# A top-k search cut into rounds: the search for the best keys is dealt out between chunks of projections, and the index scores move ahead of the first keys

## The chip, the cores and the metric

The kernel runs on one core of one Trainium2 chip. The metric is device time in microseconds (us); the time before is the median of three runs, and one further execution was recorded by the hardware profiler. The engines are PE (TensorE: matrix products, with PEld for its weight loads), DVE (VectorE), ACT (ScalarE), POOL (GpSimd) and SP (the queue that issues nearly all loads). Each engine works through its own list of instructions in order, and semaphores hold an instruction until its inputs are there. So one instruction that waits holds everything behind it on its engine.

## The reference

One decoder block on 256 tokens of 1024 channels. A normalised input is projected to queries, keys and values of 8 heads, to 8 small index heads, to the two halves of a gated mixer, and to two gates; attention looks only at the 64 best keys of each query; then follow a merge, an output projection and a mixture of 32 experts, two for each token.

```python
xn = rms_norm(h, norm1_g[l]); proj = xn @ w_in[l]
q, k, v, qi, ki, wi, su, sv, ga, gb = split_columns(proj)
...
rel = jax.nn.relu(jnp.einsum('bqhd,bsd->bqhs', qib, ki))
score = jnp.einsum('bqh,bqhs->bqs', wb, rel)             # index scores
score = jnp.where(causal[None], score, -jnp.inf)
_, sel = lax.top_k(score, top_k)                         # top_k = 64
logits = jnp.einsum('bqhd,bqkhd->bhqk', qb, kg) * (HEAD_DIM ** -0.5)
p = jax.nn.softmax(logits, axis=-1)                      # over the chosen keys
y_attn = jnp.einsum('bhqk,bqkhd->bqhd', p, vg)
...
h = h + merged @ w_out[l]
h = h + hier_moe(rms_norm(h, norm2_g[l]), ...)           # 32 experts, 2 a token
return rms_norm(h, norm_f_g)
```

## The kernel before

The weights of the first part come as 85 chunks of 512 KB or less, in one fixed order (`weight_chunks`): the index keys and index queries, the first half of the values (four pieces, v0.0 to v0.3), two pairs of key and query chunks (k0, k1, q0, q1, k2, k3, q2, q3), the second half of the values (v1.0 to v1.3), the other two pairs, and so on. Loads go through SP into four landing buffers taken in turn, so a load is issued when the chunk four places ahead of it has been read.

Products are taken at nearly full fp32 accuracy from three products of a coarser type. For that each chunk is split: ACT copies it into a rounded part (`hi`, a CAST), DVE subtracts to get the rest (`lo`, written `hl<-raw,hl` at L173 or L291). PE multiplies `hi` with the two parts of the input (L204, L205, for values L228, L229), then `lo` with the first (L209, for values L231). A key or query chunk is 16 products with `hi` and then 8 with `lo`; a piece of values is two halves of 4 and 2. There are three accumulators of PSUM for these products, used in turn.

After a pair of chunks DVE turns the accumulator by the position (`heads`: `ra`, `rs`, then two writes of `kt` or `qt`). The index side has its own: `index_queries(0)` and `(1)` (four copies `sw` on ACT, then three operations on DVE), the index products (`query_by_key` with `kip`, tile `lg<-index`, four groups for four pairs of index heads), a relu on ACT for each head (`rel`), and two fused multiply-adds on DVE for each head (`score`). Each row of the score has 256 keys, or 128 for the first 128 queries.

The search takes the 64 best by eight rounds. A round is, for each half of the tokens, MAX (the 8 largest of a row) and MATCH_REPLACE (these 8 crossed out), so four instructions on DVE (MATCH_REPLACE shows in the trace with a short load of its own). From what is crossed out comes `bias`, which masks the logits. `weights(p)` is the attention of heads 2p and 2p+1: products `lg<-kt,qt`, bias, softmax on DVE and ACT. `turn(p)` transposes the result on PE, `mix(p)` multiplies it with the values.

A scheduler orders each engine's instructions from the order of the program and its own estimate of times, so the order on an engine is not quite that of the code.

After the attention come the gates and mixer (to 260 us), the output projection, and from about 299 us the experts, whose 96 MB come through a ring of 23 buffers. Of these buffers many lie where the first part had its tiles, and can be filled only when that part is through.

Of the kernel before, what the change touches and what calls it, by code (L numbers as in the profile page):

```python
# [9 lines left out]
F32 = mybir.dt.float32  # L10
# [3 lines left out]
AF = mybir.ActivationFunctionType  # L14
ALU = mybir.AluOpType
# [10 lines left out]
IH = 8  # L26
TOPK = 64
# [9 lines left out]
DONE = -3.3e38  # L37
# [3 lines left out]
RELUS = 2  # L41
# [13 lines left out]
C_TRI, C_TRIL, C_CB, C_END = 172, 300, 428, 812  # L55
# [27 lines left out]
PIECES = 4  # L83
# [45 lines left out]
def block(ctx, tc, a, out):  # L129
    nc = tc.nc  # L130
# [41 lines left out]
    copies = []  # L172
# [40 lines left out]

    two = lambda n, p: [f"{n}{2 * p}", f"{n}{2 * p + 1}"]

    def tokens_by_cols(name, b, xs, between=None, **engines):

        accs = [ps.tile([P, BLOCK], F32, name="acc", bufs=3) for _ in range(NT)]
        for j in range(PIECES):
            piece = f"{name}{b}.{j}"  # L220
            if piece not in ready:
                prepare(piece, **engines)
            hi, lo = ready.pop(piece)
            for t in range(NT):
                s = slice(t * P, (t + 1) * P)
                ks = [(i, j * KD // PIECES + i) for i in range(KD // PIECES)]
                for i, k in ks:
                    mm(accs[t], xs[0][:, k, s], hi[:, i], start=(k == 0), stop=False)  # L228
                    mm(accs[t], xs[1][:, k, s], hi[:, i], start=False, stop=False)  # L229
                for i, k in ks:  # L230
                    mm(accs[t], xs[0][:, k, s], lo[:, i], start=False, stop=(k == KD - 1))  # L231
            if j == PIECES // 2 - 1 and between:
                between()
        return accs

    def scaled(dst, name, b, xs, scale, between=None, **engines):
# [47 lines left out]
    ident = con[:, C_ID:C_ID + P]  # L284
# [121 lines left out]
    def index_queries(j):  # L406
        ra, rs = rope64(qi_acc[j], swap(qi_acc[j], 2, P), 2, P)
        vec(nc.vector.tensor_add, qit[:, 2 * j:2 * j + 2], ra, rs)

    def values(b, between=None, **engines):  # L410

        v = at.tile([P, NT, BLOCK], F32, name="v", bufs=2)
        scaled(v, "v", b, xs, rstd1, between, **engines)
        return v

    def heads(p, what, between=None):

        acc = cols_by_tokens(two(what, p), xs, between)
        ra = sm.tile([P, 2, T], F32, name="ra", tag="ra", bufs=2)
        rs = sm.tile([P, 2, T], F32, name="rs", tag="rs", bufs=2)  # L420
        bc = lambda t: t[:, 0:1].broadcast_to([P, 2, T])
        nc.vector.tensor_mul(ra, acc, bc(cos))
        nc.vector.tensor_mul(rs, acc, bc(sin))
        o = at.tile([P, 2, T], F32, name=what + "t", tag=what, bufs=2)
        nc.vector.tensor_sub(o[:, 0], ra[:, 0], rs[:, 1])
        nc.vector.tensor_add(o[:, 1], ra[:, 1], rs[:, 0])
        return o

    v, kt, qt = {}, {}, {}
    v[0] = values(0, lambda: index_queries(0), act=act, vec=vec)  # L430
    index_queries(1)
    wi = at.tile([P, NT, IH], F32, name="wi")
    wi_ps = ps.tile([P, NT, IH], F32, name="wi_ps", tag="pt", bufs=2)
    for t in range(NT):
        nc.tensor.transpose(wi_ps[:, t], wit[:, t * P:(t + 1) * P], ident[0:IH, 0:IH])
    nc.scalar.copy(wi, wi_ps)
    kt[0] = heads(0, "k")

    pool(nc.gpsimd.tensor_copy, ident_b, ident)
    pool(nc.gpsimd.tensor_copy, bits[:, 2 * P:], early(C_TRI, 2 * P))  # L440

# [5 lines left out]
    def query_by_key(lhs, rhs):  # L447

        lgs = [ps.tile([P, 3 * P], F32, name="lg", bufs=2) for _ in range(2)]
        n, turn = lhs.shape[1], in_turn()  # L450
        for t in range(NT):
            for h in range(n):
                for j, lg in ((1, lgs[1]), (0, lgs[0])):
                    rows = slice(64 * j, 64 * j + 64)
                    turn(mm, lg[:, row[t]], lhs[rows, h, t * P:(t + 1) * P], rhs[rows, h, 0:(t + 1) * P],
                       start=(h == 0), stop=(h == n - 1), tile_position=(64 * j, 0))
        return lgs

    for hd in range(IH):
        if hd % 2 == 0:  # L460
            lgs = query_by_key(qit[:, hd // 2:hd // 2 + 1], kip)
        lg = lgs[hd % 2]
        rel = at.tile([P, 3 * P], F32, name="rel", tag="pts", bufs=2)
        ins = nc.scalar.activation(rel, lg, AF.Relu)
        if hd < RELUS:
            copies.append((order.index("k1"), ins))
        for t in range(NT):
            nc.vector.scalar_tensor_tensor(
                score[:, row[t]], rel[:, row[t]], wi[:, t, hd:hd + 1], (cb if hd == 0 else score)[:, row[t]],
                op0=ALU.mult, op1=ALU.add)  # L470

    work = at.tile([P, 3 * P], F32, name="work", tag="pr", bufs=2)
    for r in range(TOPK // 8):
        for t in range(NT):
            src = (work if r else score)[:, row[t]]
            m8 = at.tile([P, 8], F32, name="m8", bufs=2)
            nc.vector.max(m8, src)
            nc.vector.match_replace(work[:, row[t]], m8, src, DONE)
    bias = at.tile([P, 3 * P], F32, name="bias")
    nc.vector.tensor_tensor(bias, work, score, ALU.is_equal)  # L480
    nc.vector.scalar_tensor_tensor(bias, bias, -1.0e38, cb, op0=ALU.mult, op1=ALU.add)


    yah = big("y_hi", [P, H, T], "yah", F32R)
# [39 lines left out]
    def gating_values(b, between=None):
        scaled(sv[:, :, b * BLOCK:(b + 1) * BLOCK], "sv", b, xs, rstd1, between)

    qt[0] = heads(0, "q")
    kt[1] = heads(1, "k")
    qt[1] = heads(1, "q")
    weights(0)  # L530
    v[1] = values(1, lambda: turn(0))
    kt[2] = heads(2, "k", lambda: mix(0))
    weights(1)
    qt[2] = heads(2, "q")
    turn(1)
# [568 lines left out]
```

## Time and profile before

| | |
|---|---|
| median of three runs | 501.32 us (499.56 to 501.77) |
| profiled execution, its own time | 505.71 us |
| its span in the profile | 503.9 us |
| PE, DVE, ACT busy | 452.2, 220.3, 185.9 us |
| loads from memory | 148.88 MB, 298 GB/s over the span |
| mean granted clock of PE | 0.96 |

The span is from the first to the last instruction of the recorded execution. Its own time is 1.8 us more, and 4.4 us above the median of the runs that were only timed. Busy times of different engines overlap, so what counts is which engine is waited for in which stretch.

### The profile page before, as it was taken

How to read it: one execution, taken by the hardware profiler on the slowest of the kernel's cores; microseconds unless marked ns; L12 is line 12 of the kernel's file. 1: busy time of each engine (PE TensorE's matmuls, PEld its weight loads, DVE VectorE, ACT ScalarE, POOL GpSimd, SP SyncE). 2: the span in 40 equal slices, each digit the busy share in tenths (PEclk: the TensorE clock that was granted, in tenths of full speed). 3: DMA queues.
4: the chain of work that ended last, by engine and by line, in shares of the span. 5: the costliest groups of instructions: out<-in, count | busy, mean ns of one | idle time of the engine just before them, and what ended most of it. 6: DMA issues, size and time to landing. Idle time of an engine off the chain costs nothing.

```text
span 503.9 us, 8336 instructions
## 1 busy us (share of the span) xinstructions
PE 452.2 (90%) x3371; PEld 329.2 (65%) x3372; DVE 220.3 (44%) x416; ACT 185.9 (37%) x323; POOL 25.8 (5%) x50
## 2 busy tenths in 40 slices
PE   9999969999999999999999988989889887859581
PEld 8978968998878889988889963534435423214240
DVE  5587897667537546764656452012011000001012
ACT  7574317365487353544445541010100101000122
POOL 0030000000000000000001420000000000000010
PEclk9999979999999999999999999999999997978896
DMA  8676135956877999556689599999999999999942
GB/s 282 230 215 190 43 119 147 353 204 237 290 250 227 336 348 342 192 186 197 178 318 337 198 375 411 420 421 421 420 421 421 419 422 420 421 421 420 423 186 88
DMA packets 29134, 150.52 MB, mean 299 GB/s; under 512 B 3618, under 2 KB 4002, under 8 KB 16931
## 3 DMA queue, kind: packets, MB, share of 16 engines
q1 hardware_dynamic: 28512, 148.89, 78.0%
q10 hardware_dynamic: 578, 1.05, 0.7%
q8 instruction: 28, 0.46, 0.4%
q14 instruction: 16, 0.12, 0.1%
HBM read 148.88 MB, written 1.05 MB: 298 GB/s over the span
## 4 chain that ended last, share of the span: by engine, by line
PE 59%; DMA 23%; DVE 9%; ACT 6%; issue 2%; POOL 0%; POOLq 0%; DVEq 0%; ACTq 0%; SPq 0%
DMA rg<-in_ein 12%; PE acc L228 8%; PE acc L231 8%; PE acc L229 8%; DMA rg<-in_eout 8%; PE hd L901 6%; PE acc L209 5%; PE acc L204 4%; PE acc L205 4%; PE sum L291 3%; PE yp L291 3%; DMA raw_wo<-in_w 2%; PE xp L815 2%; DVE hl L173 2%; PE lg L291 1%
## 5 line engine op out<-in xcount | busy, mean ns | idle before, releaser
L901 PE MATMUL hd<-rg,xe 128*32 128x512 f32 x512 | 62.9, 612 | 13.4 <-DMA rg<-in_ein 12.5
L204 PE MATMUL acc<-xh,hl 128*128 128x256 f32 x224 | 56.7, 290 | 0.0
L205 PE MATMUL acc<-xl,hl 128*128 128x256 f32 x224 | 55.5, 285 | 0.0
L820 DVE TENSOR_TENSOR xe<-xp,g2t 128x256 f32<-128x256 f32 x32 | 12.2, 420 | 90.8 <-PE xp L815 69.2
L228 PE MATMUL acc<-hl,xh 128*128 128x512 f32 x128 | 51.0, 398 | 0.8 <-DVE ra L291 0.8
L229 PE MATMUL acc<-hl,xl 128*128 128x512 f32 x128 | 50.2, 392 | 0.0
L901 PEld LDWEIGHTS hd<-rg,xe 128*32 128x32 f32 x512 | 13.8, 110 | 47.7 <-issue 31.2
L204 PEld LDWEIGHTS acc<-xh,hl 128*128 128x128 f32 x224 | 43.4, 194 | 1.5 <-issue 1.0
L205 PEld LDWEIGHTS acc<-xl,hl 128*128 128x128 f32 x224 | 43.3, 193 | 0.5 <-issue 0.3
L291 PE MATMUL yp<-rg,aT 128*32 128x256 f32 (+1 forms) x528 | 35.3, 413 | 7.7 <-ACT aT L846 4.7
L836 ACT ACTIVATE act<-hd,r 128x256 f32<-128x256 f32 x8 | 3.8, 473 | 103.9 <-PE hd L901 103.9
L231 PE MATMUL acc<-hl,xh 128*128 128x512 f32 x128 | 39.4, 391 | 0.0
L209 PE MATMUL acc<-xh,hl 128*128 128x256 f32 x224 | 33.8, 295 | 0.0
L291 PE MATMUL sum<-ye,aT 128*128 128x512 f32 (+1 forms) x76 | 31.3, 552 | 1.8 <-ACT ye L927 1.8
L291 PEld LDWEIGHTS yp<-rg,aT 128*32 128x32 f32 x528 | 16.6, 119 | 23.2 <-issue 7.1
L209 PEld LDWEIGHTS acc<-xh,hl 128*128 128x128 f32 x224 | 30.5, 202 | 1.2 <-DVE hl L173 0.7
L815 PEld LDWEIGHTS <-hb 128*128 128x128 bf16 x384 | 21.9, 98 | 11.6 <-issue 11.2
L228 PEld LDWEIGHTS acc<-hl,xh 128*128 128x128 f32 x128 | 24.1, 188 | 6.6 <-issue 1.9
L231 PEld LDWEIGHTS acc<-hl,xh 128*128 128x128 f32 x128 | 24.0, 188 | 5.4 <-DVE hl L291 0.3
L229 PEld LDWEIGHTS acc<-hl,xl 128*128 128x128 f32 x128 | 24.1, 188 | 4.7
L837 DVE SCALAR_TENSOR_TENSOR act<-hd,r,act 128x256 f32<-128x256 f32 x8 | 3.9, 484 | 52.0 <-ACT act L836 52.0
L927 ACT COPY ye<-yp 128x512 f32<-128x512 f32 (+2 forms) x21 | 10.0, 482 | 41.0 <-PE yp L291 41.0
(263 smaller groups left out, 779.2 us busy)
## 6 DMA issues: line engine op xcount, KB each, us to landing
rg<-in_ein SPq DMA_DIRECT2D x64, 1024.0 KB, 19.8
rg<-in_eout SPq DMA_DIRECT2D x31, 1024.0 KB, 19.8
raw_v<-in_w SPq DMA_DIRECT2D x8, 512.0 KB, 3.7
raw_k<-in_w SPq DMA_DIRECT2D x8, 512.0 KB, 4.6
raw_q<-in_w SPq DMA_DIRECT2D x8, 512.0 KB, 4.4
raw_sv<-in_w SPq DMA_DIRECT2D x8, 512.0 KB, 4.1
raw_gb<-in_w SPq DMA_DIRECT2D x8, 512.0 KB, 5.0
raw_wb<-in_w SPq DMA_DIRECT2D x8, 512.0 KB, 5.7
```

What stands on the lines that cost most here:

```text
L173: plain = lambda f, *args, **kw: f(*args, **kw)
L204: mm(o, hi[:, k], xs[0][:, k], start=(k == 0), stop=False)
L205: mm(o, hi[:, k], xs[1][:, k], start=False, stop=False)
L209: mm(o, lo[:, k], xs[0][:, k], start=False, stop=(k == KD - 1))
L228: mm(accs[t], xs[0][:, k, s], hi[:, i], start=(k == 0), stop=False)
L229: mm(accs[t], xs[1][:, k, s], hi[:, i], start=False, stop=False)
L231: mm(accs[t], xs[0][:, k, s], lo[:, i], start=False, stop=(k == KD - 1))
L291: last.append(f(*args, **kw))
L815: mm(xp[:, k], hb[:, n, t, (q * 4 + k) * P:(q * 4 + k + 1) * P], s[:, t], start=(t == n == 0), stop=(t == NT - 1 and n == 2))
L820: nc.vector.tensor_mul(xe[:, ks], xp[:, k:k + 2], g2b)
L901: mm(hd[js[j]], xe[:, k, js[j]], w[:, j], start=(k == 0), stop=(k == KD - 1), tile_position=(0, j * CAP))
L927: nc.scalar.copy(ye[:, cs], yp)
```

## The change

The index scores become a function `scores(p)` for a pair of index heads, and the search a function `best(rounds)`. `values` and `tokens_by_cols` take a dictionary of what to do after which piece. The calls are then written in another order: `index_queries(0)` after piece v0.0, the index weights after v0.1, `index_queries(1)` after v0.2, the scores between v0, k0 and k1, and one or two rounds of the search between any two chunks from q0 to v1.1. The attention steps follow later by about a pair of chunks at first and catch up at the end; keys and queries get three buffers each in place of two.

```diff
-            if j == PIECES // 2 - 1 and between:
-                between()
+            if j in between:
+                between[j]()
...
-        o = at.tile([P, 2, T], F32, name=what + "t", tag=what, bufs=2)
+        o = at.tile([P, 2, T], F32, name=what + "t", tag=what, bufs=3)
...
-    v[0] = values(0, lambda: index_queries(0), act=act, vec=vec)
-    index_queries(1)
...
-    kt[0] = heads(0, "k")
...
-    for hd in range(IH):
-        if hd % 2 == 0:
-            lgs = query_by_key(qit[:, hd // 2:hd // 2 + 1], kip)
-        lg = lgs[hd % 2]
...
+    def scores(p):
+        for j, lg in enumerate(query_by_key(qit[:, p:p + 1], kip)):
+            hd = 2 * p + j
+            rel = at.tile([P, 3 * P], F32, name="rel", tag="pts", bufs=2)
+            ins = nc.scalar.activation(rel, lg, AF.Relu)
...
+    v[0] = values(0, {0: lambda: index_queries(0), 1: index_weights, 2: lambda: index_queries(1)}, act=act, vec=vec)
+    for p in (0, 1):
+        scores(p)
+    kt[0] = heads(0, "k", lambda: scores(2))
+    scores(3)
...
-    for r in range(TOPK // 8):
-        for t in range(NT):
-            src = (work if r else score)[:, row[t]]
-            m8 = at.tile([P, 8], F32, name="m8", bufs=2)
-            nc.vector.max(m8, src)
-            nc.vector.match_replace(work[:, row[t]], m8, src, DONE)
...
+    def best(rounds):
+        for r in rounds:
+            for t in range(NT):
+                src = (work if r else score)[:, row[t]]
+                m8 = at.tile([P, 8], F32, name="m8", bufs=2)
+                nc.vector.max(m8, src)
+                nc.vector.match_replace(work[:, row[t]], m8, src, DONE)
+        if r == TOPK // 8 - 1:
+            nc.vector.tensor_tensor(bias, work, score, ALU.is_equal)
+            nc.vector.scalar_tensor_tensor(bias, bias, -1.0e38, cb, op0=ALU.mult, op1=ALU.add)
...
-    qt[0] = heads(0, "q")
-    kt[1] = heads(1, "k")
-    qt[1] = heads(1, "q")
-    weights(0)
-    v[1] = values(1, lambda: turn(0))
-    kt[2] = heads(2, "k", lambda: mix(0))
+    qt[0] = heads(0, "q", lambda: best([0]))
+    best([1])
+    kt[1] = heads(1, "k", lambda: best([2]))
+    best([3])
+    qt[1] = heads(1, "q", lambda: best([4]))
+    best([5])
+    v[1] = values(1, {0: lambda: best([6]), 1: lambda: best([7]), 3: lambda: weights(0)})
+    kt[2] = heads(2, "k")
+    turn(0)
     weights(1)
-    qt[2] = heads(2, "q")
-    turn(1)
-    kt[3] = heads(3, "k", lambda: mix(1))
+    qt[2] = heads(2, "q", lambda: mix(0))
+    kt[3] = heads(3, "k", lambda: turn(1))
     weights(2)
-    qt[3] = heads(3, "q")
+    qt[3] = heads(3, "q", lambda: mix(1))
     turn(2)
     mixed = []
-    gating_values(0, lambda: mix(2))
-    weights(3)
-    gating_values(1, lambda: turn(3))
-    mixed.append(mix(3))
+    gating_values(0, {0: lambda: weights(3), 1: lambda: mix(2)})
+    gating_values(1, {0: lambda: turn(3), 2: lambda: mixed.append(mix(3))})
```

On DVE, the end of the search before (`m8` the eight largest, `work` the row being crossed out, hl_771 the `lo` of chunk k3, hl_808 that of q2):

```order
L477 MAX m8_663<-work_620 128x8
L477 MAX m8_666<-work_620 128x8
L478 MATCH_REPLACE work_620<-m8_663,work_620 128x128
L478 MATCH_REPLACE work_620<-m8_666,work_620 128x256
L422 TENSOR_TENSOR ra_734<-acc_675,cos_315 128x512
L480 TENSOR_TENSOR bias_669<-work_620,score_563 128x384
L423 TENSOR_TENSOR rs_735<-acc_675,sin_316 128x512
L481 SCALAR_TENSOR_TENSOR bias_669<-bias_669,con2_159 128x384
L425 TENSOR_TENSOR qt_738<-ra_734,rs_735 128x256
L426 TENSOR_TENSOR qt_738<-ra_734,rs_735 128x256
L173 TENSOR_TENSOR hl_771<-raw_k3_772,hl_771 128x1024
L173 TENSOR_TENSOR hl_808<-raw_q2_809,hl_808 128x1024
```

The same place on DVE now (hl_739 is the `lo` of k3, hl_782 that of q2):

```order
L484 MATCH_REPLACE work_620<-m8_733,work_620 128x128
L422 TENSOR_TENSOR ra_690<-acc_625,cos_315 128x512
L423 TENSOR_TENSOR rs_691<-acc_625,sin_316 128x512
L484 MATCH_REPLACE work_620<-m8_736,work_620 128x256
L425 TENSOR_TENSOR qt_694<-ra_690,rs_691 128x256
L426 TENSOR_TENSOR qt_694<-ra_690,rs_691 128x256
L173 TENSOR_TENSOR hl_739<-raw_k3_740,hl_739 128x1024
L483 MAX m8_775<-work_620 128x8
L483 MAX m8_778<-work_620 128x8
L484 MATCH_REPLACE work_620<-m8_775,work_620 128x128
L484 MATCH_REPLACE work_620<-m8_778,work_620 128x256
L173 TENSOR_TENSOR hl_782<-raw_q2_783,hl_782 128x1024
```

Before, all eight rounds stood ahead of the turning of q0 and q1 and of the `lo` of k3; now three rounds stand ahead of them, and the others behind, one or less between two subtractions.

On PE, the first attention products before, which stand between the `hi` products and the `lo` products of k3 and q2:

```order
L205 MATMUL acc<-xl,hl 128x256
L291 MATMUL lg<-kt,qt 128x128 x4
L291 MATMUL lg<-kt,qt 128x256 x2
L209 MATMUL acc<-xh,hl 128x256 x16
L204 MATMUL acc<-xh,hl 128x256
```

On PE now, at the end of v1 (one of the eight products of `weights(0)` stands a little earlier, in v1.1):

```order
L231 MATMUL acc<-hl,xh 128x512 x2
L291 MATMUL lg<-kt,qt 128x128 x3
L291 MATMUL lg<-kt,qt 128x256 x4
L204 MATMUL acc<-xh,hl 128x256
L205 MATMUL acc<-xl,hl 128x256
```

The first attention products moved behind q3 and the four pieces of v1, and nothing stands between `hi` and `lo` of k3 and q2 any more.

On ACT, in the first half of the values, before (raw_v0 are its pieces, `sw` the copies for the index queries):

```order
L291 CAST hl_402<-raw_v0_403 128x1024
L291 CAST hl_419<-raw_v0_420 128x1024
L291 COPY sw_436<-acc_244 32x512 x4
L291 CAST hl_445<-raw_v0_446 128x1024
L291 CAST hl_462<-raw_v0_463 128x1024
L291 COPY sw_481<-acc_336 32x512 x4
L173 CAST hl_496<-raw_k0_497 128x1024
```

And now:

```order
L291 CAST hl_404<-raw_v0_405 128x1024
L291 COPY sw_421<-acc_244 32x512 x4
L291 CAST hl_430<-raw_v0_431 128x1024
L173 CAST hl_525<-raw_k0_526 128x1024
L291 COPY wi_399<-wi_ps_447 128x16
L291 CAST hl_451<-raw_v0_452 128x1024
L291 COPY sw_468<-acc_336 32x512 x4
L291 CAST hl_477<-raw_v0_478 128x1024
```

The first copies `sw` moved ahead of piece v0.1, the second ahead of v0.3, and the CAST of k0, with the copy of the index weights, now stands ahead of pieces v0.2 and v0.3.

## Rows read from the trace of the kernel before

**Rows 1.** Windows in us: each engine's busy time, PE's clock, loads.

```profile
core 0: us, PE busy (x) PEld busy (x) DVE busy (x) ACT busy (x) POOL busy (x), PEclk, DMA share, GB/s
27.21:45.55 18.34, 17.53 (x100) 14.69 (x98) 13.56 (x14) 11.18 (x16) 3.03 (x3) 1.00 0.71 208
45.55:54.63 9.08, 8.92 (x58) 6.26 (x57) 7.23 (x17) 3.85 (x8) 0.00 (x0) 1.00 0.42 124
...
64.26:68.27 4.01, 0.12 (x2) 0.03 (x1) 4.01 (x13) 0.00 (x0) 0.00 (x0) 0.91 0.00 0
68.27:77.67 9.40, 9.40 (x57) 8.29 (x57) 7.21 (x10) 2.62 (x3) 0.00 (x0) 0.68 0.66 214
77.67:89.52 11.85, 11.85 (x57) 9.74 (x56) 9.58 (x17) 9.50 (x20) 0.00 (x0) 1.00 0.49 141
...
150.00:260.00 110.00, 110.00 (x597) 95.65 (x596) 66.84 (x75) 55.53 (x66) 0.89 (x2) 1.00 0.75 256
...
374.00:475.00 101.00, 78.31 (x734) 33.04 (x734) 9.92 (x28) 8.96 (x17) 1.84 (x3) 0.91 1.01 421
```

**Rows 2.** Timeline of PE: start, duration, line, tile, count, [idle before, releaser].

```profile
56.54 1.12 PE L209 MATMUL acc<-xh,hl 128*128 128x256 f32 x8
...
59.42 1.12 PE L209 MATMUL acc<-xh,hl 128*128 128x256 f32 x8
...
68.27 2.08 PE L291 MATMUL lg<-kt,qt 64*128 64x128 f32 x12 [3.89 <-DVE qt L425]
70.28 3.78 PE L209 MATMUL acc<-xh,hl 128*128 128x256 f32 x16
```

**Rows 3.** Timeline of DVE from the last scores to the subtractions behind the search.

```profile
54.86 1.40 DVE L468 SCALAR_TENSOR_TENSOR score<-rel,wi,score 128x128 f32<-128x128 f32 x4 [1.07 <-ACT rel L464]
56.18 0.61 DVE L477 MAX8 m<-score 128x8 f32<-128x128 f32 x2
...
65.57 0.69 DVE L422 TENSOR_TENSOR ra<-acc,cos 128x512 f32<-128x512 f32 x1
66.17 0.56 DVE L480 TENSOR_TENSOR bias<-work,score 128x384 f32<-128x384 f32 x1
...
67.70 0.42 DVE L425 TENSOR_TENSOR qt<-ra,rs 128x256 f32<-128x256 f32 x1
...
68.37 1.23 DVE L173 TENSOR_TENSOR hl<-raw_k,hl 128x1024 fp32r<-128x1024 f32 x1
69.50 2.36 DVE L173 TENSOR_TENSOR hl<-raw_q,hl 128x1024 fp32r<-128x1024 f32 x2
```

**Rows 4.** Timeline of PE around the first group of index products.

```profile
44.59 1.12 PE L209 MATMUL acc<-xh,hl 128*128 128x256 f32 x8
45.64 0.93 PE L291 MATMUL lg<-index 64*128 64x128 f32 x8
46.50 0.38 PE L204 MATMUL acc<-xh,hl 128*128 128x256 f32 x1
```

**Rows 5.** Timeline of PE in the first half of the values.

```profile
30.68 0.47 PE L228 MATMUL acc<-hl,xh 128*128 128x512 f32 x1 [0.81 <-DVE ra L291]
...
37.58 0.61 PE L231 MATMUL acc<-hl,xh 128*128 128x512 f32 x2
...
38.94 0.61 PE L231 MATMUL acc<-hl,xh 128*128 128x512 f32 x2
```

**Rows 6.** SP issues k0 and k1; landing of k0 alone; the page's median.

```profile
28.16 2.00 SPq L167 DMA_DIRECT2D raw_k<-in_w  x2
...
DMA to landing us min/median/max: 3.5/3.5/3.5
...
raw_k<-in_w SPq DMA_DIRECT2D x8, 512.0 KB, 4.6
```

**Rows 7.** Timeline of ACT: four copies for the index queries, and one CAST.

```profile
33.42 2.35 ACT L291 COPY sw<-acc 32x512 f32<-32x512 f32 x4
...
47.37 1.05 ACT L173 CAST hl<-raw_k 128x1024 fp32r<-128x1024 f32 x1
```

More of the change, by code (lines that the diff above doesn't have):

```diff
@@ L214, in block, with tokens_by_cols @@
     two = lambda n, p: [f"{n}{2 * p}", f"{n}{2 * p + 1}"]
-    def tokens_by_cols(name, b, xs, between=None, **engines):
+    def tokens_by_cols(name, b, xs, between={}, **engines):
         accs = [ps.tile([P, BLOCK], F32, name="acc", bufs=3) for _ in range(NT)]
@@ L231, in tokens_by_cols, with scaled @@
                     mm(accs[t], xs[0][:, k, s], lo[:, i], start=False, stop=(k == KD - 1))
-            if j == PIECES // 2 - 1 and between:
-                between()
+            if j in between:
+                between[j]()
         return accs
-    def scaled(dst, name, b, xs, scale, between=None, **engines):
+    def scaled(dst, name, b, xs, scale, between={}, **engines):
         for t, acc in enumerate(tokens_by_cols(name, b, xs, between, **engines)):
@@ L408, in index_queries, with values @@
         vec(nc.vector.tensor_add, qit[:, 2 * j:2 * j + 2], ra, rs)
-    def values(b, between=None, **engines):
+    def values(b, between={}, **engines):
         v = at.tile([P, NT, BLOCK], F32, name="v", bufs=2)
@@ L427, in heads, with index_weights @@
         return o
-    v, kt, qt = {}, {}, {}
-    v[0] = values(0, lambda: index_queries(0), act=act, vec=vec)
-    index_queries(1)
     wi = at.tile([P, NT, IH], F32, name="wi")
-    wi_ps = ps.tile([P, NT, IH], F32, name="wi_ps", tag="pt", bufs=2)
-    for t in range(NT):
-        nc.tensor.transpose(wi_ps[:, t], wit[:, t * P:(t + 1) * P], ident[0:IH, 0:IH])
-    nc.scalar.copy(wi, wi_ps)
-    kt[0] = heads(0, "k")
-    pool(nc.gpsimd.tensor_copy, ident_b, ident)
-    pool(nc.gpsimd.tensor_copy, bits[:, 2 * P:], early(C_TRI, 2 * P))
+    def index_weights():
+        wi_ps = ps.tile([P, NT, IH], F32, name="wi_ps", tag="pt", bufs=2)
+        for t in range(NT):
+            nc.tensor.transpose(wi_ps[:, t], wit[:, t * P:(t + 1) * P], ident[0:IH, 0:IH])
+        act(nc.scalar.copy, wi, wi_ps)
     row = (slice(0, P), slice(P, 3 * P))
@@ L457, in query_by_key @@
         return lgs
-    for hd in range(IH):
-        if hd % 2 == 0:
-            lgs = query_by_key(qit[:, hd // 2:hd // 2 + 1], kip)
-        lg = lgs[hd % 2]
[L463 to L470, printed above, removed]
@@ L472, in block @@
-    work = at.tile([P, 3 * P], F32, name="work", tag="pr", bufs=2)
-    for r in range(TOPK // 8):
-        for t in range(NT):
-            src = (work if r else score)[:, row[t]]
-            m8 = at.tile([P, 8], F32, name="m8", bufs=2)
-            nc.vector.max(m8, src)
-            nc.vector.match_replace(work[:, row[t]], m8, src, DONE)
-    bias = at.tile([P, 3 * P], F32, name="bias")
-    nc.vector.tensor_tensor(bias, work, score, ALU.is_equal)
-    nc.vector.scalar_tensor_tensor(bias, bias, -1.0e38, cb, op0=ALU.mult, op1=ALU.add)
+    def scores(p):
[3 more added lines that the diff above has]
+            ins = nc.scalar.activation(rel, lg, AF.Relu)
+            if hd < RELUS:
+                copies.append((order.index("k1"), ins))
+            for t in range(NT):
+                nc.vector.scalar_tensor_tensor(
+                    score[:, row[t]], rel[:, row[t]], wi[:, t, hd:hd + 1], (cb if hd == 0 else score)[:, row[t]],
+                    op0=ALU.mult, op1=ALU.add)
@@ new lines, in block @@
+    v, kt, qt = {}, {}, {}
+    v[0] = values(0, {0: lambda: index_queries(0), 1: index_weights, 2: lambda: index_queries(1)}, act=act, vec=vec)
[3 more added lines that the diff above has]
+    scores(3)
+    pool(nc.gpsimd.tensor_copy, ident_b, ident)
+    pool(nc.gpsimd.tensor_copy, bits[:, 2 * P:], early(C_TRI, 2 * P))
+    work = at.tile([P, 3 * P], F32, name="work", tag="pr", bufs=2)
+    bias = at.tile([P, 3 * P], F32, name="bias")
+    def best(rounds):
+        for r in rounds:
+            for t in range(NT):
+                src = (work if r else score)[:, row[t]]
[5 more added lines that the diff above has]
+            nc.vector.scalar_tensor_tensor(bias, bias, -1.0e38, cb, op0=ALU.mult, op1=ALU.add)
@@ L522, in block, with gating_values @@
     sv = big("m_hi", [P, NT, D], "sv")
-    def gating_values(b, between=None):
+    def gating_values(b, between={}):
         scaled(sv[:, :, b * BLOCK:(b + 1) * BLOCK], "sv", b, xs, rstd1, between)
-    qt[0] = heads(0, "q")
-    kt[1] = heads(1, "k")
-    qt[1] = heads(1, "q")
-    weights(0)
-    v[1] = values(1, lambda: turn(0))
-    kt[2] = heads(2, "k", lambda: mix(0))
+    qt[0] = heads(0, "q", lambda: best([0]))
[7 more added lines that the diff above has]
+    turn(0)
     weights(1)
-    qt[2] = heads(2, "q")
-    turn(1)
-    kt[3] = heads(3, "k", lambda: mix(1))
+    qt[2] = heads(2, "q", lambda: mix(0))
+    kt[3] = heads(3, "k", lambda: turn(1))
     weights(2)
-    qt[3] = heads(3, "q")
+    qt[3] = heads(3, "q", lambda: mix(1))
     turn(2)
     mixed = []
-    gating_values(0, lambda: mix(2))
-    weights(3)
-    gating_values(1, lambda: turn(3))
-    mixed.append(mix(3))
+    gating_values(0, {0: lambda: weights(3), 1: lambda: mix(2)})
+    gating_values(1, {0: lambda: turn(3), 2: lambda: mixed.append(mix(3))})
     ta.close()
```

## Prediction

> **What bounds the kernel now.** I read the windows first, to find the stages and their limits. In the last long one, 374 to 475 us, the DMA engines are full (share 1.01, 421 GB/s) and PE is not (78 of 101 us): the experts' weights set that end. From 150 to 260 us it is the other way: PE is busy for all 110 us and loads run at 256 GB/s, so they wait for buffers that PE's progress frees [rows 1]. A microsecond won on PE before 150 us therefore moves everything behind it, the start of the full stream too.
>
> So I looked for what PE loses before 90 us. There is one hole: from 64.26 to 68.27 PE has 0.12 us of work, while DVE is busy for all 4.01 us [rows 1]. In PE's timeline the hole ends with the products `lg<-kt,qt`, released by the write of `qt` on DVE [rows 2]. DVE's timeline says why `qt` is late: from 56.18 to 65.57 it does nothing but the eight rounds, 9.39 us, and the turning of q0 and q1 and the subtractions for k3 and q2 stand behind them [rows 3]. The hole has a tail: in the 9.40 us behind it the granted clock is 0.68 [rows 1], and sixteen `lo` products take 3.78 us where eight took 1.12 [rows 2].
>
> **What is removed.** Four terms, all on PE.
> - The hole: 4.0 us.
> - The slow clock behind it: 9.40 x (1 - 0.68) = 3.0 us. It was at the lower level (1.2 in place of 2.4 GHz) for most of that stretch, after the idle, and came back with work.
> - Scattered index products. Between the last `lo` product ahead of the first group (44.59 + 8 x 0.12 = 45.55) and the next chunk's first product at 46.50 lie 0.95 us [rows 4]: one group in one piece. A chunk takes 59.42 - 56.54 = 2.88 us [rows 2]. Four groups and one chunk should take 4 x 0.95 + 2.88 = 6.7 us; the window 45.55 to 54.63 holds just these and took 9.08 [rows 1]: 2.4 us lost, since three groups are cut up among the products of q0.
> - The 0.81 us that PE waited in v0 for the index queries to leave their accumulator [rows 5].
>
> Together 10.2 us: the most that this change can give.
>
> **What is added.** No instruction is new, so the price is in waits; I followed the new lists with the durations of the rows.
>
> *First half of the values* (two steps of 1.36 us make a piece of 2.72 [rows 5]). The second accumulator of v0 is free once the index queries' multiplications are through: about 0.25 us of waiting at 28.6, where 0.81 was. The subtraction of v0.1 now stands behind these three operations: 0.25 at 31.2. Then ACT. Its CAST of k0 stands ahead of that of v0.2. The load of k0 is issued at 28.16 and landed 3.5 us later [rows 6], so the CAST (1.05 us [rows 7]) is over at 32.7; the copy of the index weights waits for their transposes on PE, to 33.7; v0.2 is ready at 34.8. PE has the weights and one index group to do meanwhile, to 34.5: 0.3 us of waiting. If k0 took the median of 4.6 us [rows 6], it would be 0.5. Then the four copies `sw`, 2.35 us [rows 7], stand ahead of v0.3: ready at 38.2, wanted at 37.75, so 0.45. Together 1.25 us. The load of q1 now waits for the subtraction of v0.3, near 40.7; its CAST then ends near 46, ahead of relus wanted by PE at 48.2, so this is covered; were it 2 us later, the next index group would wait that long.
>
> *The search.* Before, DVE's list held eight rounds in one block; now its work from the end of k1 must keep pace with PE. In my count k1 ends at 48.2 on PE and DVE is free at 48.55. Until the `lo` of v1.0 stands: three turnings at 0.60 x 2 for `ra`, `rs` and 0.67 for the writes (66.17 - 65.57 and 68.37 - 67.70), five subtractions at 1.13 (69.50 - 68.37), four multiply-adds at 0.33 (56.18 - 54.86 for four), six rounds at 9.39 / 8 = 1.17 [rows 3]: 5.6 + 5.65 + 1.3 + 7.0 = 19.6 us, that is 68.2. PE does one index group and six chunks, 0.95 + 17.3 us, to 66.5, and wants that `lo` after four products, 0.9 us on: it waits 0.8. For q3 the same count gives 0.25, for k3, q2 and the other pieces of v1 0.1 or less. Together 1.1 us. Here DVE and PE have almost the same amount of work, so any delay of DVE is PE's.
>
> How a round fares when it is cut by other instructions the trace does not show. Below, it could be free of cost, even with the waits of 1.1 gone. Above, I take one wait like the 1.07 us for the relu [rows 3] at each of two places, 2.1 us, and the clock falling once, 3.0. I take no extra, since within the block each instruction already followed the one it needs.
>
> *Pieces.* The second index group is split 3 + 1, and the products of `weights(1)` are cut by transposes: 0.3 us each, estimated from the 2.4 us lost on three cut groups. `weights(0)` goes from 6 + 2 to 1 + 7: nothing. SP issues the same loads; only k2's stands ahead of q0's and some expert pieces one load earlier. That is covered by four landing buffers: PE takes 4 x 2.88 us to come round to one. The later `weights`, `turn` and `mix` still have two chunks or pieces between softmax and transposes: nothing.
>
> Sum: 10.2 - 1.25 - 1.1 - 0.6 = 7.2 us; I say 7.0. The profiled execution would go from 505.71 to 498.7 us, its span from 503.9 to 496.9. The median of the runs lies 4.4 us below the profiled one, so 501.3 - 7.0 = **494.3 us**.
>
> **Rivals.**
> 1. *The hole moves to v1.* The rounds cost DVE 9.4 us as before, and in 48 to 77 us it has no room. If its list is late by 2 us or more at v1.0, PE stands still there and its clock may fall again. The same hole and clock over again would leave 10.2 - 7.0 - 1.25 - 0.6 = 1.3 us: 500.0; 2.1 us more of waiting without the clock, 496.4. For it: the 0.8 us wait found above. Against it: in the old block DVE never waited, and its durations are from there. 0.20.
> 2. *The gain does not reach the end*, because the experts' stream sets it: 501.3. Against it: the loads before 260 us run at 256 GB/s with PE never idle [rows 1], so the stream starts when PE lets it. 0.06.
> 3. *Slower: the clock falls on short waits.* There are now six waits of 0.25 to 0.8 us in my count. Each fall costs about 3.0 us, as behind the old hole. With two falls the time is 500.3; from three on the gain is gone (503.3), four make 506.3. Against it: after the 0.81 us wait at 30 us the clock stayed at 1.00 up to 45.55 [rows 1, 5]. The Trainium skill's page "TensorE: Matmul & The Clock Gate" (A second HAM failure mode) tells of frequent short idles between groups of matmuls that make the clock swing between half and full. By that rule the time would be the 506.3 of this rival; the trace agrees so far only for the long hole. 0.08.
>
> **How the numbers follow.** My case has 0.60, 492 to 497. The remaining 0.06 are delays that I did not see, some us either way. What a measurement of this kernel can tell from no change is about 0.5%, 2.5 us. Faster than 498.8: 0.60, under half of rival 1 (0.08), some of the rest: 0.70. Within: the rest of rival 1, rival 2, part of rival 3: 0.19. Slower than 503.8: 0.11. The range starts at 491.5, where nearly all of the 10.2 us come, and ends at 500.5, which takes in rival 1 and leaves out rival 3 and the unchanged time.
>
> **What would show it.** Right: no idle of PE above 1 us between 27 and 90 us, a clock of 1.00 there, the end of v1 some 10 us earlier than 89.5 (3 us of that only because the first attention products and transposes come later), and PE's 110 busy us of the gates shifted by 7 us as a block, with the stream at 421 GB/s as long as before. Wrong: PE waiting for `hl` on DVE in q3 to v1 by more than 2 us, or for ACT in v0 by more than 1; a clock under 1 in these windows; or the shift there at 150 us and gone at 475.

## The result, and the profile after

The changed kernel takes 496.59 us (median of 16 runs, 492.65 to 499.45); before takes 501.01 beside it. The ratio is 0.9908, 95% interval 0.9881 to 0.9935: 0.9% faster. The ratio leaves out one slow run of before, of 659.37 us. This ratio and those below are not the quotients of the two medians, from which they differ by up to 0.3%. In a later set of runs (e5 below) the ratio is 0.9843 (0.9793 to 0.9894), 494.52 against 501.51 us. The profiled execution of the changed kernel took 495.49 us. First its span, and the windows that answer to [rows 1]; the columns are the same.

```profile
core 0: 493.7 us, clock 0.965
```

```profile
27.21:45.55 18.34, 16.88 (x92) 12.06 (x91) 12.50 (x18) 11.12 (x17) 0.95 (x2) 1.00 0.58 180
64.26:68.27 4.01, 3.63 (x27) 3.10 (x25) 4.01 (x11) 1.94 (x2) 0.00 (x0) 1.00 0.50 171
68.27:77.67 9.40, 9.22 (x40) 7.34 (x41) 9.40 (x23) 3.11 (x3) 0.00 (x0) 1.00 0.55 176
27.00:140.00 113.00, 110.36 (x722) 94.93 (x721) 84.83 (x173) 62.05 (x113) 1.16 (x2) 1.00 0.63 214
140.00:250.00 110.00, 110.00 (x597) 95.65 (x596) 65.84 (x73) 56.51 (x67) 0.89 (x2) 1.00 0.75 257
364.00:465.00 101.00, 82.08 (x764) 33.95 (x761) 10.58 (x31) 8.73 (x17) 2.47 (x4) 0.92 1.01 421
```

The hole is gone: PE is busy for 3.63 of the 4.01 us that had 0.12 before, and the clock is 1.00 from 27 to 140 us. DVE is full in both windows now (before, it was busy for 7.21 of the 9.40 us of the second); its work is the same, and PE waits for it much less. The 110 us in which PE is never idle stand 10 us earlier, and the stream moves 421 GB/s as before.

The spans differ by 10.2 us (503.9 and 493.7), more than the timed medians. To see why, the next rows give three marks in PE's timeline, first of before: the transposes of the index scale (`r_ps`), ahead of anything that the change touches; the first `hi` product of k3; and the first product `mt`, near the end of the gates. Between the last two stand three waits of the transposes `pt` (idle before and releaser in brackets).

```profile
23.18 0.60 PE L380 MATMUL r_ps<-scr,ones 128*128 128x256 f32 x2
60.38 0.28 PE L204 MATMUL acc<-xh,hl 128*128 128x256 f32 x1
...
104.77 0.84 PE L508 MATMUL pt<-con,pr 128*128 128x128 f32 x3 [0.35 <-ACT pr L501]
120.81 0.84 PE L508 MATMUL pt<-con,pr 128*128 128x128 f32 x3 [0.35 <-ACT pr L501]
141.85 0.84 PE L508 MATMUL pt<-con,pr 128*128 128x128 f32 x3 [0.42 <-ACT pr L501]
...
243.10 1.08 PE L622 MATMUL mt<-con,mb 128*128 128x128 f32 x8
```

The same marks of the changed kernel, with the four longest waits of PE between them.

```profile
20.89 0.60 PE L380 MATMUL r_ps<-scr,ones 128*128 128x256 f32 x2
...
31.54 0.93 PE L291 MATMUL lg<-index 64*128 64x128 f32 x8
33.67 0.50 PE L228 MATMUL acc<-hl,xh 128*128 128x512 f32 x1 [1.20 <-ACT hl L291]
36.93 0.35 PE L204 MATMUL acc<-xh,hl 128*128 128x256 f32 x1 [0.23 <-DVE ra L291]
...
58.14 0.28 PE L204 MATMUL acc<-xh,hl 128*128 128x256 f32 x1
...
68.45 0.73 PE L231 MATMUL acc<-hl,xh 128*128 128x512 f32 x2 [0.56 <-DVE hl L173]
...
79.28 0.93 PE L291 MATMUL lg<-kt,qt 64*128 64x128 f32 x9
...
116.75 1.60 PE L291 MATMUL lg<-kt,qt 64*128 64x128 f32 x16 [0.62 <-DVE qt L425]
...
234.39 1.08 PE L628 MATMUL mt<-con,mb 128*128 128x128 f32 x8
```

The changed execution is 2.3 us ahead at `r_ps` already (20.89 and 23.18), where the lists of PE, ACT and DVE are still the same in both kernels. So I count from there. Up to k3: 37.20 us before, 37.25 after, no gain at all. From k3 to `mt`: 182.72 before, 176.25 after, 6.5 us. That is what the change gives in the trace, 6.4 us in all. Behind `mt` 260.8 us were left of the span before and 259.3 after (258.3 to 259.8 and 257.9 in the later profiles of the two kernels), so the gain reaches the end.

The same marks for all profiles (us; the columns "to k3" and "k3 to mt" for those that the argument needs; each ratio is to before in its own set of runs):

| kernel | r_ps at | to k3 | k3 to mt | r_ps to mt | ratio to before, timed |
|---|---|---|---|---|---|
| before | 23.18 | 37.20 | 182.72 | 219.92 | 1 |
| changed | 20.89 | 37.25 | 176.25 | 213.50 | 0.9908 |
| e1 scores ahead only | 20.21 | 37.18 | 181.68 | 218.86 | 0.9965 |
| e2 rounds and order only | 20.13 | 37.22 | 176.10 | 213.32 | 0.9871 |
| e3 changed, search in one block | 20.51 | 37.21 | 178.39 | 215.60 | 0.9947 |
| e4 changed, CAST of k0 later | 22.07 | 36.20 | 176.32 | 212.52 | 0.9863 |
| e5 changed again | 22.04 | | | 213.53 | 0.9843 |
| e6 before, kept warm | 21.83 | | | 217.69 | 0.9979 |
| e7 e4, one round later | 21.52 | | | 211.71 | 0.9842 |
| e8, e10, e12 before again | 23.73, 23.27, 23.25 | | | 220.01, 219.97, 219.95 | |
| e9 changed, MAX twice | 20.08 | | | 214.49 | 0.9908 |
| e11 e3 again | 23.40 | | | 216.67 | |

### The profile page after: what moved, and what is told of

Its sections match the earlier page's. It is cut to its first block, busy times and chain, and to the rows that moved or that the text cites. A ratio compares the mean times of both kernels' runs of the same rounds, so it can differ in the third digit from the quotient of the medians.

```text
span 493.7 us, 8330 instructions
## 1 busy us (share of the span) xinstructions
PE 448.6 (91%) x3371; PEld 323.7 (66%) x3372; DVE 219.6 (44%) x416; ACT 185.8 (38%) x323; POOL 26.0 (5%) x50
## 3 DMA queue, kind: packets, MB, share of 16 engines
q10 hardware_dynamic: 578, 1.05, 0.7%
HBM read 148.88 MB, written 1.05 MB: 304 GB/s over the span
## 4 chain that ended last, share of the span: by engine, by line
PE 72%; DMA 13%; DVE 7%; ACT 4%; issue 2%; POOL 0%; SPq 0%; POOLq 0%; DVEq 0%; ACTq 0%
PE acc L231 9%; PE acc L229 8%; PE acc L228 8%; DMA rg<-in_eout 8%; PE hd L907 8%; PE yp L291 6%; PE acc L204 6%; PE acc L205 5%; PE acc L209 5%; PE sum L291 5%; DMA rg<-in_ein 4%; PE xp L821 3%; PE lg L291 2%; DVE hl L173 1%; DMA xg<-in_xg 1%
## 5 line engine op out<-in xcount | busy, mean ns | idle before, releaser
L204 PE MATMUL acc<-xh,hl 128*128 128x256 f32 x224 | 56.3, 289 | 0.2 <-DVE ra L291 0.2
L204 PEld LDWEIGHTS acc<-xh,hl 128*128 128x128 f32 x224 | 42.8, 191 | 2.7 <-issue 1.7
L291 PE MATMUL yp<-rg,aT 128*32 128x256 f32 (+1 forms) x528 | 38.6, 443 | 5.8 <-ACT aT L852 4.7
L291 PEld LDWEIGHTS yp<-rg,aT 128*32 128x32 f32 x528 | 18.1, 126 | 23.7 <-issue 7.8
L291 PE MATMUL sum<-ye,aT 128*128 128x512 f32 (+1 forms) x76 | 30.3, 537 | 1.8 <-ACT ye L933 1.8
L209 PE MATMUL acc<-xh,hl 128*128 128x256 f32 x224 | 31.8, 284 | 0.0
L209 PEld LDWEIGHTS acc<-xh,hl 128*128 128x128 f32 x224 | 29.0, 192 | 0.1
```

Of the source, the lines that this page charges most:

```text
L204: mm(o, hi[:, k], xs[0][:, k], start=(k == 0), stop=False)
L209: mm(o, lo[:, k], xs[0][:, k], start=False, stop=(k == KD - 1))
L291: last.append(f(*args, **kw))
```

## The experiments

The first four, e1 to e4, ran in one set, where before took 502.90 us (median of 23 runs).

**e1: the scores ahead, and nothing else.** The search is one block again, and the attention steps have their old order.

```diff
-    qt[0] = heads(0, "q", lambda: best([0]))
-    best([1])
...
+    best(range(TOPK // 8))
+    qt[0] = heads(0, "q")
+    kt[1] = heads(1, "k")
+    qt[1] = heads(1, "q")
+    weights(0)
...
```

> Only the index queries and scores are moved ahead of the first keys; the search is one block of eight rounds again and the attention steps stand in their old order. My theory (the hole came from the search in one block): the hole and its slow clock (7.0 us) stay, and of the gain only the scattered products (2.4) and the wait in v0 (0.8) less the new waits of v0 (1.25) and the split group (0.3) is left, 1.7 us: ratio about 0.997, a hole of 3 to 5 us on PE between hi and lo of k3 or q2. Rival (the hole came from the late scores, and the search would have fitted in, had it begun earlier): no hole above 1 us, and a ratio near 0.991 as for the whole change.

Measured: 500.74 us, ratio 0.9965 (0.9935 to 0.9996). PE's timeline:

```profile
64.33 2.08 PE L291 MATMUL lg<-kt,qt 64*128 64x128 f32 x12 [2.93 <-DVE qt L425]
66.33 3.78 PE L209 MATMUL acc<-xh,hl 128*128 128x256 f32 x16
```

The hole is there, 2.93 us in place of 3.89, with the slow products behind it. So moving the scores does not remove it. The rest of the expectation fell: up to k3 nothing is won (37.18), and of the 1.1 us gained 0.96 come from the shorter hole: the search begins 32.0 us behind `r_ps`, and 33.0 before.

**e2: the rounds and the attention order, and nothing else.** Index queries, weights and scores stand where they stood before.

```diff
-    v[0] = values(0, {0: lambda: index_queries(0), 1: index_weights, 2: lambda: index_queries(1)}, act=act, vec=vec)
-    for p in (0, 1):
+    v[0] = values(0, {1: lambda: index_queries(0)}, act=act, vec=vec)
+    index_queries(1)
...
+    kt[0] = heads(0, "k")
+    for p in range(4):
...
```

> The index queries and scores stay in their old place, with groups scattered among the products of q0; the search goes by rounds and the attention steps stand in the new order. My theory: hole and slow clock are gone (7.0 us), the 2.4 us of scattered products and the 0.8 us wait stay, waits of the search stage (1.1) and the cut weights(1) (0.3) are added: 5.6 us gained, ratio 0.989, or less by what DVE, which gets the scores some 2 us later, then comes late for v1 (2 us late: 3.6 us gained, 0.993). Rival (the scores' place matters and the rounds do not): ratio 0.998 or above, with the hole moved to v1.

Measured: 495.46 us, ratio 0.9871 (0.9823 to 0.9918). From `r_ps` to `mt` it takes 213.32 us, the whole change 213.50. So the rounds with the new order of the attention steps give all of it, 6.6 us, and moving the scores ahead adds nothing to them. The two go together: `weights(0)` needs the mask of the last round, so rounds that reach into v1 push it behind them. No run deals out the rounds in the old order.

**e3 and e11: the changed kernel with the search in one block**, two profiles of one kernel (e11 for the clock, below).

```diff
-    qt[0] = heads(0, "q", lambda: best([0]))
-    best([1])
-    kt[1] = heads(1, "k", lambda: best([2]))
...
+    qt[0] = heads(0, "q", lambda: best(range(TOPK // 8)))
+    kt[1] = heads(1, "k")
...
```

> As the changed kernel, but the eight rounds stand in one block behind the first chunk of q0. If the dealing out of the rounds is what removed the hole, it is back here, 3 to 5 us with a slow clock behind it, since the writes of the first turned queries and the lo of k3 and q2 stand behind the block: 5 to 7 us slower than the changed kernel, ratio to before about 1.00. Rival (the later attention steps removed the hole, and the rounds might as well stay in a block): ratio about 0.991, as for the whole change.

> e3 once more, for its profile: the hole is 2.9 us again. If the fall of the clock is a matter of chance behind such a hole, this run may show it (218.5 us from r_ps to mt) where e3 did not (215.6). If it depends on the order of the products (e3 has no product of keys and queries behind v1, e1 has), 215.6 again.

Measured: e3 498.83 us, ratio 0.9947 (0.9915 to 0.9979). The hole is back at 2.93 us, with the attention steps in their new order, so it is the dealing out of the rounds that removes it. From `r_ps` to `mt` it costs 2.1 us against the changed kernel in e3 and 3.2 in e11, not 5 to 7: the hole is 2.93 us long, the wait of 0.56 us at v1.0 is gone in exchange, and the clock fell in e11 only. PE's timeline and clock of e3 (windows of 2 us), then of e11, then the clock of e1:

```profile
64.65 1.17 PE L291 MATMUL lg<-kt,qt 64*128 64x128 f32 x12 [2.93 <-DVE qt L425]
66.03 2.34 PE L209 MATMUL acc<-xh,hl 128*128 128x256 f32 x16 [0.21 <-DVE hl L173]
...
66.00:68.00 2.00, 1.97 (x15) 1.84 (x16) 2.00 (x2) 0.72 (x1) 0.00 (x0) 1.00 0.47 102
68.00:70.00 2.00, 2.00 (x19) 2.00 (x18) 2.00 (x4) 0.58 (x2) 0.00 (x0) 1.00 0.90 277
```

```profile
67.57 1.90 PE L291 MATMUL lg<-kt,qt 64*128 64x128 f32 x12 [2.93 <-DVE qt L425]
69.39 2.97 PE L209 MATMUL acc<-xh,hl 128*128 128x256 f32 x16
...
68.00:70.00 2.00, 2.00 (x13) 1.35 (x12) 2.00 (x3) 0.00 (x0) 0.00 (x0) 0.50 0.08 12
70.00:72.00 2.00, 2.00 (x14) 2.00 (x14) 1.71 (x3) 0.55 (x1) 0.00 (x0) 0.69 0.79 270
```

```profile
64.00:66.00 2.00, 1.68 (x12) 1.39 (x12) 2.00 (x4) 0.00 (x0) 0.00 (x0) 0.50 0.00 0
...
68.00:70.00 2.00, 2.00 (x11) 2.00 (x11) 1.56 (x3) 1.05 (x1) 0.00 (x0) 0.50 0.86 311
```

One kernel, one hole of 2.93 us: the granted clock stayed at the upper level in e3 and fell to the lower in e11, which cost 216.67 - 215.60 = 1.1 us (I had forecast 218.5 with the fall). The length of the idle alone does not decide it. In e11 the clock rises again between 70 and 72 us; in e1, behind a hole of the same length, it is 0.50 from 64 to 70 us, and the `lo` products there take 3.78 us where e11 needs 2.97.

**e4: the CAST of k0 behind that of v0.3.**

```diff
     v[0] = values(0, {0: lambda: index_queries(0), 1: index_weights, 2: lambda: index_queries(1)}, act=act, vec=vec)
+    prepare("k0", act, vec)
```

> As the changed kernel, but the CAST of k0 is put behind that of v0.3 on ACT. If the wait of 1.2 us on PE in v0, with ACT as its releaser, comes from that CAST standing ahead of v0.2, it goes to 0.3 or less, and the time falls by about 0.9 us (0.2%) against the changed kernel: ratio to before 0.989. Rival (v0.2 would be late anyway, behind the copies of the index queries): the wait stays at 1 us or more, or moves to k0, whose lo then comes late; the ratio stays at 0.991.

Measured: 495.73 us, ratio 0.9863 (0.9816 to 0.9910). In the changed kernel ACT's list in v0 reads:

```profile
31.43 1.04 ACT L173 CAST hl<-raw_k 128x1024 fp32r<-128x1024 f32 x1 [5.12 <-PE acc L231]
32.50 0.17 ACT L291 COPY wi<-wi_ps 128x16 f32<-128x16 f32 x1
32.57 1.05 ACT L291 CAST hl<-raw_v 128x1024 fp32r<-128x1024 f32 x1
```

ACT stood idle for 5.12 us in front of k0's CAST, with v0.2 waiting behind it. These rows tell what it waited for: k0's load (one load, issued at 25.88), and PE at the end of v0.1.

```profile
L167 SPq DMA_DIRECT2D raw_k<-in_w x1: 328/328/328, 25.9 to 25.9; - x1
DMA to landing us min/median/max: 3.6/3.6/3.6
...
30.78 0.61 PE L231 MATMUL acc<-hl,xh 128*128 128x512 f32 x2
```

The load landed at 29.5, and the CAST began at 31.43, when PE's last products of v0.1 ended (30.78 + 0.61 = 31.39), as the releaser in the view says. The code gives the reason: `hl` has three buffers, taken in turn in the order of the program (v0.0, v0.1, v0.2, v0.3, k0), so k0 gets the buffer of v0.1 and must wait until PE has read that piece. In e4 ACT and PE show

```profile
32.86 0.17 ACT L291 COPY wi<-wi_ps 128x16 f32<-128x16 f32 x1 [5.38 <-PE wi_ps L435]
...
34.02 0.50 PE L228 MATMUL acc<-hl,xh 128*128 128x512 f32 x1 [0.35 <-ACT hl L291]
37.47 0.50 PE L228 MATMUL acc<-hl,xh 128*128 128x512 f32 x1 [0.30 <-ACT hl L291]
```

and k3 is reached 1.05 us earlier than in the changed kernel (36.20 against 37.25). So the place of k0's CAST is shown as the cause of most of the wait. ACT still stands idle, for 5.38 us, now for the products of the index weights, which come behind v0.1 on PE; that the 0.35 us left come from their copy is likely, but was not tested. In the timed runs such a size cannot be told apart.

The next four, e5 to e8, ran in a later set, where before took 501.51 us (median of 17 runs).

**e5: the changed kernel again**, unchanged.

> The changed kernel again, beside the next two on one chip. The start up to the transposes of the index scale differs by up to 3 us between the profiles so far, so stages are counted from there (the first product r_ps). If the change gives what the first pair of profiles showed, 213.5 us from there to the first product mt, where before took 219.9, this one takes 213.5 within 0.5 again, with a wait of 1.2 us in v0 and of 0.6 at v1.0; ratio about 0.991. Rival (the profile pair was a lucky draw): a stretch off by 1 us or more.

Measured: 494.52 us (493.23 to 495.90), ratio 0.9843. From `r_ps` to `mt` 213.53 us, as in the first profile (213.50), with waits of 1.20 and 0.55 us at the same two places.

**e6: before, with PE kept busy in the hole.** Dummy products of zeros stand behind the `hi` products of q2.

```diff
...
+        if p == 0:
+            y = ps.tile([P, 2, T], F32, name="y", bufs=1)
+            with tc.issue_after(last_hi["q2"].ins):
+                for _ in range(32):
+                    mm(y[:, 0, 0:P], zero, zero, start=True, stop=True)
```

> The kernel before, with 32 dummy products of zeros (0.11 us each by the start of the profile, 3.6 us) between the hi products of q2 and the first products of keys and queries, where PE stood idle for 3.9 us. The hole stays, but PE is busy in it. Theory 1 (the clock falls behind the hole in every execution, as in the profile before): no lower clock here, 3.0 us gained, ratio 0.994. Theory 2 (after one and the same hole the clock falls in some executions only: behind 2.9 us of idle it fell in e1 and stayed at 1.00 in e3): the gain is a part of 3.0 us, ratio 0.996 to 0.998, with the lowest times as before and the highest gone. Theory 3 (the clock plays no part in the times): 1.000.

Measured: 500.48 us (12 runs, 498.42 to 502.02), ratio 0.9979 (0.9945 to 1.0012).

```profile
62.88 1.96 PE L496 MATMUL y<-zero 128*128 128x128 bf16 x32
66.92 1.17 PE L293 MATMUL lg<-kt,qt 64*128 64x128 f32 x12 [2.08 <-DVE qt L427]
68.30 2.36 PE L211 MATMUL acc<-xh,hl 128*128 128x256 f32 x16 [0.21 <-DVE hl L173]
```

The 32 products took 0.06 us each, not 0.11, so 2.08 us of idle remain; the sixteen `lo` products behind take 2.36 us in place of 3.78 [rows 2]. Against before, `r_ps` to `mt` falls by 219.92 - 217.69 = 2.2 us: this is the price of the clock behind the hole, where I had 3.0. So the clock does play a part (theory 3 fails in the trace), with a smaller price than theory 1 has. In the timed runs the gain is unclear (the interval holds 1), though the highest times are gone: before went up to 506.09 in this set.

**e7: as e4, with one round fewer ahead of v1.0.**

```diff
-    best([5])
-    v[1] = values(1, {0: lambda: best([6]), 1: lambda: best([7]), 3: lambda: weights(0)})
+    v[1] = values(1, {0: lambda: best([5]), 1: lambda: best([6]), 2: lambda: best([7])})
+    weights(0)
```

> As e4, but three rounds in place of two are dealt out in v1, so that five and not six stand ahead of its first piece, and the first attention products follow at its end. The wait at v1.0 (0.56 us, for a lo of DVE) came since DVE's list, which has no idle from the end of k1 on, held one round too many ahead of it. If so, that wait goes, and the stretch from r_ps to mt falls from 212.5 (e4) to 212.0 us; ratio 0.986 to 0.990. Rival: the round moved makes the bias late, and the attention products wait for 1 us or more: 213 or above.

Measured: 494.84 us, ratio 0.9842 (0.9786 to 0.9897). The wait at v1.0 went and one of 0.38 us came at v1.1. From `r_ps` to `mt` 211.71 us, 0.8 less than e4 and 1.8 less than the changed kernel: the shortest of all here. The waits make up 0.2 of the 0.8; the first attention products also stand in one piece now, but that the rest comes from this was not tested. The timed medians of e5 and e7 (494.52 and 494.84) don't tell them apart.

**e8, e10 and e12: before, three more profiles.**

> The kernel before once more, for its profile: the hole is 3.9 us again. If the clock behind it is a matter of chance, it may stay at 1.00 here, and the stretch from r_ps to mt is then 217 us, where the first profile had 219.9; if it falls each time, 219.9 within 0.5.

> The kernel before for a third profile. Both so far had a start of 23.2 to 23.7 us up to r_ps and a low clock behind the hole, and both lie at 505 us, where the timed runs lie at 498.6 to 506.1. Theory 2 of e6 (the fall is a matter of chance) allows a clock of 1.00 behind the hole and 217.7 us from r_ps to mt, as in e6; theory 1 gives 219.9 again.

> The kernel before for a fourth profile. In three out of three the start took 23.2 to 23.7 us, and the clock fell behind the hole of 3.9 us, with 219.9 to 220.0 us from r_ps to mt. If the fall is a matter of chance behind this hole too, as e3 and e11 showed it behind 2.9 us, it may be absent here: 217 to 218 us. If a hole of 3.9 us is long enough for it each time, 219.9 again, and the spread of the times of before comes from its start and its end.

Measured: 505.29, 503.76 and 503.25 us. In all four profiles of before the clock fell behind the hole of 3.89 or 3.90 us, and `r_ps` to `mt` agrees within 0.1 us. The clock in e12, windows of 2 us:

```profile
66.00:68.00 2.00, 0.00 (x0) 0.00 (x0) 2.00 (x5) 0.00 (x0) 0.00 (x0) 0.90 0.00 0
68.00:70.00 2.00, 1.63 (x12) 1.39 (x12) 2.00 (x4) 0.00 (x0) 0.00 (x0) 0.50 0.00 0
70.00:72.00 2.00, 2.00 (x10) 1.62 (x8) 1.96 (x2) 0.00 (x0) 0.00 (x0) 0.50 0.59 160
```

So behind 3.9 us it fell four times in four, behind 2.9 us in e1 and e11 and not in e3. That before runs at times without the fall, as I supposed, is not shown.

**e9: the changed kernel, each MAX done twice**, for 4.2 us more of DVE.

```diff
                 nc.vector.max(m8, src)
+                nc.vector.max(at.tile([P, 8], F32, name="m8x", bufs=2), src)
```

> As the changed kernel, with each MAX of the search done twice (the second into a tile that nobody reads): DVE gets 0.53 us more in each of eight rounds, 4.2 us in all, 3.2 of it ahead of the lo of v1.0. If DVE's list has no slack there (my count, and rival 1 of the prediction: any delay of DVE is PE's), PE waits 3 us or more longer between q2 and v1.2 and the clock falls again behind the longest wait: the stretch from r_ps to mt goes from 213.5 to 216.5 us, or to 219 with the clock; ratio 0.993 to 0.997. Rival (rounds fit into slack of DVE): under 1 us of new waits, ratio as for the changed kernel, 0.985 to 0.991.

Measured: 495.83 us, ratio 0.9908 (0.9875 to 0.9942), beside before at 500.33 (13 runs). From `r_ps` to `mt` 214.49 us, 1.0 more than the changed kernel. The new waits (that of 0.56 us at v1.0 is gone):

```profile
59.94 1.22 PE L209 MATMUL acc<-xh,hl 128*128 128x256 f32 x8 [0.23 <-DVE hl L173]
...
74.99 1.19 PE L231 MATMUL acc<-hl,xh 128*128 128x512 f32 x4 [1.02 <-DVE hl L173]
```

The `lo` of v1.0 is ready 50.2 us behind `r_ps` here and 47.5 in the changed kernel, 2.6 us later, from these rows of DVE, first e9's and then the changed kernel's:

```profile
69.03 1.20 DVE L173 TENSOR_TENSOR hl<-raw_v,hl 128x1024 fp32r<-128x1024 f32 x1
```

```profile
67.18 1.22 DVE L173 TENSOR_TENSOR hl<-raw_v,hl 128x1024 fp32r<-128x1024 f32 x1
```

PE loses little by it, and its list is another one too: the scheduler knew of the longer DVE list and put `hi` products of the next chunks and the first attention products ahead of the late `lo` products. My count, and the rival's point that any delay of DVE is PE's, fell: of 4.2 us more, 1.0 reach PE. What a late DVE would cost with PE's list unchanged was not tested.

## Why the prediction was right, and where its terms were off

- **Direction, mechanism and time** held: 494.3 predicted, 496.59 and (in e5) 494.52 measured, both inside 491.5 to 500.5. The gain of 7.0 us that I said stands against 6.4 in the profiles, and 4.4 and 7.0 between the timed medians; the interval of the first set (3.3 to 6.0 us) leaves 7.0 out, that of e5 (5.3 to 10.4) takes it in. The difference between the two sets I can't explain. That the sum came so near is in part luck: the stretch up to k3 and the clock gave 2.5 us less together than I had counted, and other places 1.7 us more. One sign that I had named for being right is absent: PE has an idle of 1.20 us, where I said none above 1.
- **The hole and the clock** (4.0 + 3.0): the hole term is right, by e1, e3 and e11, where the block of rounds brings it back. The clock term was too large, 2.2 us by e6. I took the missing share of the clock, 0.32 of 9.40 us, as lost time. But at 0.50 the products did not take twice as long: 2.08 us against 1.17 in e6 for the first attention products, and 3.78 against 2.36 for the `lo` products, 1.8 and 1.6 times as long.
- **Up to k3**, "Four groups and one chunk should take 6.7 us ... 2.4 us lost" together with "Together 1.25 us" of new waits: this is the step that was mis-sized most. I counted 2.4 + 0.8 won against 1.25 + 0.3 lost, 1.7 us; the marks show 0.0. The scattered products did shrink: by PE's timeline the four index groups take 4.1 us where they took 6.2. But v0 takes 13.9 us without the groups that now lie in it, 12.3 before, so 1.6 us more, and the five chunks behind it 0.4 more. In v0 PE waits 1.20 and 0.23 us where it waited 0.81; what goes beyond these waits lies in gaps too short to be listed as idle. The wait of 1.20 us is where the working failed: I let k0's CAST begin when its load had landed, 3.5 us after the issue. The landing was right (3.6 us), but the CAST had to wait about 2 us more for the buffer of v0.1, and so v0.2 kept PE waiting for 1.20 us where I had 0.3. I had named a wait for ACT of more than 1 us in v0 as a sign of being wrong, and for this term it was: e4 takes 1.05 us of it back with one line.
- **From k3 on** I counted 7.0 won against 1.1 + 0.3 lost, 5.6 us; it was 6.5, although the clock gave 0.8 less. Of the 0.8 us wait at v1.0 came 0.56, of the 0.25 at q3 nothing. And "The later `weights`, `turn` and `mix` ... nothing" missed a gain: before, PE waits three times for transposes behind the softmax, 0.35 + 0.35 + 0.42 = 1.1 us, and the changed kernel once, 0.62 us, for turned queries at 116.75. This goes with the order of the attention steps: e1 and e6, in the old order, have the three waits, e2 and e3, in the new one, only the other. The remaining 0.7 us (the 0.3 of cut pieces that I took off, and 0.4 more) I can't place.
- **Rival 1** (the hole moves to v1) did not come, and e9 shows more distance from it than I saw, with a list on PE made for it. **Rival 2** (no gain at the end): refuted, the part behind `mt` keeps its length (260.8 and 259.3 us). **Rival 3** (short waits bring the clock down): refuted in these profiles, 1.00 from 27 to 140 us with waits of 1.20, 0.62 and 0.56 us in it. The rule of the Trainium skill's page "TensorE: Matmul & The Clock Gate" (A second HAM failure mode) that I had set beside it does not show here.

## What to carry to other kernels

A long block on one engine that nobody needs soon, ahead of short steps that another engine waits for, can be dealt out between these steps, with what needs its result moved behind it. Here the two together gave all of the gain (e2); with the block back in one piece 2.1 to 3.2 of the 6.4 us were lost again (e3, e11), and the rest stayed: a hole 1 us shorter than before, less or no slow clock behind it, and the new order of the attention steps. Even 4.2 us more of such work cost only 1.0, with the list of the waiting engine reordered around it. Count stages from a mark ahead of the change: the two spans differed by 10.2 us, of which 2.3 lay in front of anything changed. When a step is moved ahead, look at what it waits for besides its data, and at what stands behind it on its engine: here a CAST came to stand in front of another one while the buffer that it writes was still being read.

## What the runs showed of the hardware

- Behind the same idle of 2.93 us in the same kernel the clock fell once and stayed up once (e11 and e3). Where it fell it cost 1.1 us (e11 against e3), and behind the hole of 3.9 us 2.2 us (before against e6).
- At a granted clock of 0.50 the first attention products took 1.8 times and the `lo` products 1.6 times as long as at 1.00, not twice (before against e6).
- The start differs from run to run too. The rows are a product of the index keys in the first profile of before and of the changed kernel:

```profile
7.88 0.41 PE L324 MATMUL acc<-xh,hl 128*72 128x256 f32 x1
```

```profile
7.06 0.28 PE L324 MATMUL acc<-xh,hl 128*72 128x256 f32 x1
```

The lists of PE, DVE and ACT are the same in all kernels here up to `r_ps`. Of the 90 products `acc` ahead of it, 26 to 28 took 0.41 us or more in the four profiles of before and in e11, which reach `r_ps` at 23.2 to 23.7 us; 14 or 15 did in e4 to e7 (21.5 to 22.1 us), and one or none in the changed kernel's first profile, e1, e2, e3 and e9 (20.1 to 20.9 us). The page "TensorE: Matmul & The Clock Gate" of the Trainium skill (Part 1: The HAM clock gate) says that the number of slow products at a kernel's start varies from run to run; these profiles agree. That all four profiles of before fell into the slowest group may be chance: e6, whose lists are the same there, did not.
